# Input norms from token rows on ScalarE, an early spread of the bias table with a late read, and memory keys and values evacuated later

## The chip, the core and the metric

The kernel runs on one core of a Trainium2 chip. The metric is the time of one execution on the device, in microseconds (us), as a median of several runs. The engines are TensorE (PE, with PEld for its weight loads), VectorE (DVE), ScalarE (ACT), GpSimd (POOL) and SyncE (SP), whose queue issues nearly all DMAs here.

## What is computed

Two layers of an encoder trunk over 256 tokens of width 2048, in float32:

```
for l in range(DEPTH):                       # DEPTH = 2
    h = rms_norm(x, norm_mix[l])
    proj = h @ w_in[l]                       # 10 blocks of 512 columns and 32 gate columns
    gla_out = gla_mixer(g_q, g_k, g_v, g_r, gates)
    dil_out = dilated_mixer(d_q, d_k, d_v, rel_table)        # relative bias from a table (32, 4)
    kv = rms_norm(mem, mem_norm[l]) @ w_mem_kv[l]            # memory keys and values, 512 columns each
    mem_out = memory_mixer(m_q, kv)
    x = x + concat(gla_out, dil_out, mem_out) @ w_out[l]
    h = rms_norm(x, norm_mlp[l])
    x = x + square(relu(h @ w_up[l])) @ w_down[l]            # hidden width 8192
return rms_norm(x, norm_final)
```

The factor 1 / rms belongs to a token, so it can be applied to a product after the matmul; the kernel does so when it moves products out of PSUM (L257, `evac`).

## The kernel before

Every product with a weight block of 512 columns is one call of `linear` (L221). It goes through the 2048 rows of the weights in four quads of 512 rows. A quad is loaded as a tile `raw` of 1 MB (L211, three buffers), ScalarE casts it to a high part `wh` (L232), VectorE subtracts that to get the low part `wl` (L233; four buffers of half a quad for each part), and 24 matmuls follow (L250 to L252), 96 in one call. So the load of a quad goes out when the low part of the quad three before it is done, and the casts run at most two quads ahead of TensorE.

The order of the first layer's start: gains; quads of transposed memory `memT`, each split into `mem0qh` and `mem0ql` (L154, L155), between the quads of `w_mem` block 0 (memory keys); then `w_mem` block 1 (memory values); then `w_in` block 9 (memory queries), block 0, block 1 and so on. The transposed input `xT` is loaded and split the same way (L196, planned by L552). `ColumnNorm` (L104) gets 1 / rms from these transposed quads: GpSimd squares each (L113), adds them up (L115, L120), four matmuls against a vector of ones add over partitions (L122), and GpSimd takes the power (L83). `RowNorm` (L86) does it from token rows: ScalarE squares 512 columns of 128 tokens with a running sum (L95).

The relative-bias table: a matmul makes `rows`, 4 heads on 4 partitions (L284). `late_constants` (L287) is called after `w_in` block 0 and is queued on SP behind that block's last quad. It loads `ident`, `tri` and `masks`, writes `rows` 128 times for each head to the DRAM tensor `scr` (L295), and reads it back skewed into `bt` (L303). The whole of `x` by tokens is loaded behind it in one DMA (L593).

The program is ordered by a scheduler that goes by priority in the order of tracing; `tc.issue_after(ins)` queues what is traced in it behind `ins` on that engine. Each engine, and SP's queue, runs its instructions in the order that is so fixed. Tiles of one tag are handed out in the order of tracing: `xT` tiles share the ring with `km`, and come after it.

Of the kernel before, what the change touches and what calls it, by code (L numbers as in the profile page):

```python
# [11 lines left out]
F32 = mybir.dt.float32  # L12
# [3 lines left out]
ALU = mybir.AluOpType  # L16
AX = mybir.AxisListType
PSUM = bass.MemoryType.PSUM
# [24 lines left out]
def trunk_kernel(ctx: ExitStack, tc: tile.TileContext, a: dict):  # L43
# [23 lines left out]
    ones = const.tile([P, 1], F32, name="ones")  # L67
    nc.gpsimd.memset(neghalf, -0.5)
    nc.gpsimd.memset(ones, 1.0)
# [16 lines left out]
    class RowNorm:  # L86
        """Sums of squares by chunks of 512 columns, then 1 / rms of every token."""
# [16 lines left out]
    class ColumnNorm:  # L104
        """1 / rms of every token of a transposed input."""

        def __init__(self, name):
            self.name = name
            self.sums = slot([4, S], "sums_" + name)

        def add(self, q, v):
            o = self.sums if q == 0 else slot([4, S], "sq_" + self.name)
            nc.gpsimd.tensor_tensor(o, v, v, ALU.mult)  # L113
            if q:
                nc.gpsimd.tensor_tensor(self.sums, self.sums, o, ALU.add)  # L115

        def done(self):
            ps, v = aux([NT], "ss_" + self.name), self.sums
            for n in (2, 1):
                nc.gpsimd.tensor_tensor(v[:, :n], v[:, :n], v[:, n:2 * n], ALU.add)  # L120
            for t in range(NT):
                nc.tensor.matmul(  # L122
                    ps[:, t:t + 1], v[:, 0, t * P:(t + 1) * P], ones, start=True, stop=True
                )
            ss = small.tile([P, NT], F32, tag="ss2", name="ss_" + self.name)
            nc.vector.tensor_copy(ss, ps)
            return rstd(ss, NT, D, self.name)

    def turn_blocks(o, v):
        """o[f, kk, token] = v[token % 128, token // 128, 128 * kk + f], by blocks of 32 x 32"""  # L130
        src = v.rearrange("p t (b c) -> p t b c", b=4)
        dst = o.rearrange("p b (t s) -> p t b s", t=NT)
        for f in range(0, P, 32):
            for s in range(0, P, 32):
                yield nc.vector.transpose(
                    dst[f:f + 32, :, :, s:s + 32], src[s:s + 32, :, :, f:f + 32]
                )
# [24 lines left out]
    def split_T(v, quad, gain, name):  # L162
        """v: [P, NT, 512] of tokens; its transpose times gain, in two float32r parts"""
        h, l = new_parts(name)
        for j2 in range(2):
            ps = aux([2, S], name + "ps")
            for j in range(2):
                c = (2 * j2 + j) * P
                for t in range(NT):
                    nc.tensor.transpose(ps[:, j, t * P:(t + 1) * P], v[:, t, c:c + P], ident)  # L170
            parts_of(h, l, ps, j2, quad, gain)
        return h, l

    def split_turned(v, quad, gain, name, lhs, steps=(0, 8, 8)):
        """The same on DVE, in steps that run between the splits of weights."""
        o = turned_slot(name + "o")
        yield from paced(turn_blocks(o, v), steps)
        h, l = new_parts(name)
        for j2 in range(2):
            parts_of(h, l, o[:, 2 * j2:2 * j2 + 2, :], j2, quad, gain)  # L180
        lhs[quad] = h, l

    def heads_turned(v, name, heads):
        """The transpose alone, of all heads."""
        o = slot([H, S], name)
        yield from paced(turn_blocks(o, v), (0, 4, 4, 4, 4))
        heads[name] = o

    def turn(n=None):
        """Emits the next steps of the transposes on DVE."""  # L190
        while turning and n != 0:
            if next(turning[0], True):
                turning.popleft()
            n = n and n - 1

    def split_loaded(v, src, quad, gain, name, lhs, norm=None, pieces=1):  # L196
        """The parts of an input that lies transposed in memory; v is where it is loaded to."""
        n = 4 // pieces
        for c in range(0, 4, n):
            nc.sync.dma_start(v[:, c:c + n], src[quad, :, c:c + n])  # L200
            yield
        h, l = new_parts(name)
        for j2 in range(2):
            parts_of(h, l, v[:, 2 * j2:2 * j2 + 2, :], j2, quad, gain)
        lhs[quad] = h, l
        if norm is not None:
            norm.add(quad, v)
# [13 lines left out]
    def linear(wsrc, lhs, quads, loaded=()):  # L221
        """lhs: dict quad -> (hi, lo); returns the PSUM tiles of both token tiles."""
        ps = [ps_mm.tile([P, NW], F32, tag="mm", name=f"mm{t}") for t in range(NT)]
# [62 lines left out]

    def late_constants():  # L287
        nc.sync.dma_start(ident, a["ident"])
        tri32 = work.tile([P, 4, 320], F32, tag="E", name="tri32")
        nc.sync.dma_start(tri32, a["tri"])  # L290
        nc.vector.tensor_copy(tri, tri32)
        masks32 = slot([2, H, P], "masks32", mybir.dt.int32)
        nc.sync.dma_start(masks32, a["masks"])
        nc.vector.tensor_copy(masks, masks32)
        nc.sync.dma_start(  # L295
            scr[:, :, :NW], rows.rearrange("h (o j) -> h o j", o=1).to_broadcast([H, P, NW])
        )
        for h in range(H):
            v = bass.AP(
                tensor=scr.tensor, offset=scr.offset + h * P * SKEW + P - 1,  # L300
                ap=[[SKEW - 1, P], [1, S + P]],
            )
            nc.sync.dma_start(bt[:, h, :], v)  # L303

    def attend_weights(qT, kT, bias, name):
        """The softmax over the 256 keys, not yet divided by its sums, keys on partitions."""
# [33 lines left out]
    def attend_out(weights, v, name):  # L340
        """The attention's sum over the values, then the per-head RMS norm; [P, NT, 512]."""
# [80 lines left out]
    def gla_weights(qT, kT, gates):  # L422
# [3 lines left out]
        for d in range(2):  # L426
            qd = slot([NT, H, P], f"qd{d}")
            cr = slot([2, H, P], f"cr{d}")
            for i in range(NT):
# [24 lines left out]
                # the side that is a source of the other half holds keys, the other queries  # L454
# [22 lines left out]
                # forward blocks go where the sum is wanted, backward ones are added to them  # L477
# [55 lines left out]
    mem_norm, xnorm = ColumnNorm("mem"), ColumnNorm("mix")  # L533
    loaded, splits = [], {}
    for q in range(4):
# [3 lines left out]
            turned_slot(f"mem0{q}"), a["memT"], q, gains[:, 3, 0, :], f"mem0{q}", mem_lhs, mem_norm, n  # L539
# [5 lines left out]
        if q == 0:  # L545
            next(splits[key], None)
        else:
            pending.append(lambda key=key: next(splits[key], None))
    nc.sync.dma_start(rel, a["rel"])
    nc.sync.dma_start(onehot, a["onehot"])  # L550

    def plan_loads(name, loads, src, gain, lhs, norm=None):  # L552
        """Loads some quads after each of the next quads of weights, and splits one."""

        def step(i):
            for q in loads[i] if i < len(loads) else ():
                splits[name, q] = split_loaded(
                    slot([4, S], f"{name}{q}"), src, q, gain, f"{name}{q}", lhs, norm
# [9 lines left out]
    for l in range(DEPTH):  # L568
        w = a["w_in"]
        ps = linear(a["w_mem"][l, 0], mem_lhs, range(4), loaded if l == 0 else ())  # L570
        if l == 0:
            flush()
            bias_products()
            mem_rs = mem_norm.done()
            plan_loads("x0", ((0, 1), (2,), (3,)), a["xT"], gains[:, 0, 0, :], xlhs, xnorm)
        km = evac(ps, mem_rs, f"km{l}")
        heads = {}
        turning.append(split_turned(km, "km", None, f"kmT{l}", heads, (0, 4, 4, 4, 4)))
        ps = linear(a["w_mem"][l, 1], mem_lhs, range(4))
        vm = evac(ps, mem_rs, f"vm{l}")  # L580
        col = lambda i: linear(w[l, i], xlhs, range(4))
        ps = col(9)
        flush()
        rs = xnorm.done()
        rsq = small.tile([P, NT], F32, tag="rsq", name="rsq")
        nc.vector.tensor_scalar(rsq, rs, scale, None, ALU.mult)
        mq = evac(ps, rsq, "mq")
        turning.append(split_turned(mq, "mq", None, f"mqT{l}", heads))
        gq = evac(col(0), rsq, "gq")
        if l == 0:  # L590
            with tc.issue_after(newest[0]):
                late_constants()
                nc.sync.dma_start(x, a["x"].rearrange("(t p) d -> p t d", p=P))  # L593
# [3 lines left out]
        gk = evac(col(1), rs, "gk")  # L597
# [117 lines left out]
def _constants():  # L715
# [5 lines left out]
    # row r is a gate's position, a column an exponent's: sums over the gates between  # L721
# [18 lines left out]
def _blocks(w, width):  # L740
    """[L, K, N] -> [L, N / width, 128, K / 128, width]"""
# [6 lines left out]
def _turned(v):  # L748
    """[1, S, D] -> [D / 512, 128, 4, S]"""
# [47 lines left out]
```

## Time and profile before

| | us |
|---|---|
| median of 3 runs (2260.66 to 2263.08) | 2260.94 |
| span of the profiled execution | 2262.0 |
| TensorE busy in it | 2200.8 (97%) |
| VectorE busy | 1618.6 (72%) |
| ScalarE busy | 1124.2 (50%) |
| GpSimd busy | 71.1 (3%) |

A busy TensorE is not TensorE at its peak, since matmuls are pipelined: the records of neighbouring matmuls overlap. The distance between their starts is what one costs. Where an engine sits idle, the profile names what ended the idle time.

### The profile page before, as it was taken

How to read it: one execution, taken by the hardware profiler on the slowest of the kernel's cores; microseconds unless marked ns; L12 is line 12 of the kernel's file. 1: busy time of each engine (PE TensorE's matmuls, PEld its weight loads, DVE VectorE, ACT ScalarE, POOL GpSimd, SP SyncE). 2: the span in 40 equal slices, each digit the busy share in tenths (PEclk: the TensorE clock that was granted, in tenths of full speed). 3: DMA queues.
4: the chain of work that ended last, by engine and by line, in shares of the span. 5: the costliest groups of instructions: out<-in, count | busy, mean ns of one | idle time of the engine just before them, and what ended most of it. 6: DMA issues, size and time to landing. Idle time of an engine off the chain costs nothing.

```text
span 2262.0 us, 25763 instructions
## 1 busy us (share of the span) xinstructions
PE 2200.8 (97%) x9906; PEld 1823.4 (81%) x9906; DVE 1618.6 (72%) x2234; ACT 1124.2 (50%) x1497; POOL 71.1 (3%) x78
## 2 busy tenths in 40 slices
PE   7849999999999999999999999999999999999998
PEld 5638888888888888888888888888888888888886
DVE  7827787888567557657987677888864864765774
ACT  5426456555345445445654554655543543543543
POOL 4200000000000000000000000000000000000000
PEclk9979999999999999999999999999999999999999
DMA  6554445555555555555665443555555555555563
GB/s 250 166 161 150 168 146 171 189 202 186 198 193 188 203 186 196 195 188 203 211 206 195 170 153 135 178 186 191 194 194 201 188 191 199 186 201 190 189 220 130
DMA packets 62502, 421.16 MB, mean 186 GB/s; under 512 B 6923, under 2 KB 8203, under 8 KB 13356
## 3 DMA queue, kind: packets, MB, share of 16 engines
q1 hardware_dynamic: 62380, 419.53, 54.8%
q8 instruction: 77, 1.26, 0.2%
q14 instruction: 45, 0.37, 0.1%
HBM read 416.35 MB, written 3.15 MB: 185 GB/s over the span
## 4 chain that ended last, share of the span: by engine, by line
PE 95%; DMA 2%; DVE 2%; issue 0%; ACT 0%; SPq 0%; POOL 0%; ACTq 0%; POOLq 0%; DVEq 0%
PE mm L251 30%; PE mm L252 30%; PE mm L250 30%; DMA raw<-in_w_in 2%; DVE wl L233 1%; PE pv L350 1%; PE go L506 1%; PE pT L336 0%; DMA mem<-in_memT 0%; PE dg L466 0%; PE cum L435 0%; DVE x01l L155 0%; PE dg L470 0%; PE cum L436 0%; DVE x00l L155 0%
## 5 line engine op out<-in xcount | busy, mean ns | idle before, releaser
L233 DVE TENSOR_TENSOR wl<-raw,wh 128x1024 fp32r<-128x1024 f32 (+1 forms) x774 | 938.4, 1227 | 550.1 <-ACT wh L232 545.1
L232 ACT ACTIVATE wh<-raw 128x1024 fp32r<-128x1024 f32 (+1 forms) x774 | 814.3, 1054 | 889.8 <-PE mm L252 800.3
L252 PE MATMUL mm<-wh,uT0h 128*128 128x512 f32 x256 | 99.7, 389 | 0.0
L252 PE MATMUL mm<-wh,uT2h 128*128 128x512 f32 x256 | 99.7, 389 | 0.0
L252 PE MATMUL mm<-wh,zT1h 128*128 128x512 f32 x256 | 99.7, 389 | 0.0
L251 PE MATMUL mm<-wl,zT2h 128*128 128x512 f32 x256 | 99.7, 389 | 0.0
L251 PE MATMUL mm<-wl,uT3h 128*128 128x512 f32 x256 | 99.7, 389 | 0.0
L251 PE MATMUL mm<-wl,uT2h 128*128 128x512 f32 x256 | 99.7, 389 | 0.0
L252 PE MATMUL mm<-wh,zT0h 128*128 128x512 f32 x256 | 99.7, 389 | 0.0
L252 PE MATMUL mm<-wh,uT3h 128*128 128x512 f32 x256 | 99.7, 389 | 0.0
L251 PE MATMUL mm<-wl,zT0h 128*128 128x512 f32 x256 | 99.6, 389 | 0.0
L252 PE MATMUL mm<-wh,uT1h 128*128 128x512 f32 x256 | 99.6, 389 | 0.0
L251 PE MATMUL mm<-wl,uT0h 128*128 128x512 f32 x256 | 99.6, 389 | 0.0
L250 PE MATMUL mm<-wh,zT0l 128*128 128x512 f32 x256 | 99.6, 389 | 0.0
L252 PE MATMUL mm<-wh,zT3h 128*128 128x512 f32 x256 | 99.6, 389 | 0.0
L251 PE MATMUL mm<-wl,zT3h 128*128 128x512 f32 x256 | 99.6, 389 | 0.0
L250 PE MATMUL mm<-wh,zT1l 128*128 128x512 f32 x256 | 99.6, 389 | 0.0
L251 PE MATMUL mm<-wl,zT1h 128*128 128x512 f32 x256 | 99.6, 389 | 0.0
L251 PE MATMUL mm<-wl,uT1h 128*128 128x512 f32 x256 | 99.6, 389 | 0.0
L252 PE MATMUL mm<-wh,zT2h 128*128 128x512 f32 x256 | 99.6, 389 | 0.0
L250 PE MATMUL mm<-wh,uT1l 128*128 128x512 f32 x256 | 99.5, 389 | 0.0
L250 PE MATMUL mm<-wh,uT3l 128*128 128x512 f32 x256 | 99.3, 389 | 0.0
(447 smaller groups left out, 4721.6 us busy)
## 6 DMA issues: line engine op xcount, KB each, us to landing
raw<-in_w_up SPq DMA_DIRECT2D x128, 1024.0 KB, 4.9
raw<-in_w_down SPq DMA_DIRECT2D x128, 1024.0 KB, 4.9
raw<-in_w_in SPq DMA_DIRECT2D x80, 1024.0 KB, 5.0
raw<-in_w_out SPq DMA_DIRECT2D x32, 1024.0 KB, 4.9
raw<-in_w_mem SPq DMA_DIRECT2D x13, 1024.0 KB, 5.0
mem<-in_memT SPq DMA_DIRECT2D x7, 512.0 KB, 5.8
raw<-in_w_mem SPq DMA_DIRECT2D x12, 256.0 KB, 6.3
x<-in_xT SPq DMA_DIRECT2D x4, 512.0 KB, 6.7
```

Source lines behind the costliest of these rows:

```text
L232: nc.scalar.activation(hi, raw[:, k:k + n], AF.Copy)
L233: cut = nc.vector.tensor_tensor(lo, raw[:, k:k + n], hi.bitcast(F32), ALU.subtract)
L250: nc.tensor.matmul(ps[t], xl[:, kk, sl], hi, start=first, stop=False)
L251: nc.tensor.matmul(ps[t], xh[:, kk, sl], lo, start=False, stop=False)
L252: nc.tensor.matmul(ps[t], xh[:, kk, sl], hi, start=False, stop=last)
L350: nc.tensor.matmul(ps[:, h, :], pT[s][:, h, t * P:(t + 1) * P], v[:, s, h * P:(h + 1) * P], start=s == 0, stop=s == NT - 1,)
L506: nc.tensor.matmul(ps[:, j, :], AT[s][:, t, 2 * c + j, :], v[c][:, s, j * DV:(j + 1) * DV], start=s == 0, stop=s == NT - 1,)
```

## The change

- `ColumnNorm` and its vector of ones are gone. Both input norms of the first layer are a `RowNorm`. Memory by tokens is a new input, loaded in four DMAs of 512 columns into the tile of `x`, behind the last piece of the third quad of `w_mem` block 0; `ident` follows. ScalarE squares each chunk, and a DMA on GpSimd's queue then loads the same chunk of `x` over it; ScalarE squares that too.
- The quads of `memT` take tiles of the ring in place of two buffers of their own.
- `w_mem` block 1 accumulates in the other PSUM pool. The memory keys and values are evacuated after `w_in` block 9, the memory queries after block 0; `xT` loads are planned ahead of block 1 of `w_mem`, as before, but `km` is no longer traced in front of them.
- The write of `scr` (`spread_bias`) is queued on SP behind the last quad of `w_mem` block 1. `late_constants` keeps `tri`, `masks` and the reads of `bt`.
- In both layers the memory attention is traced behind `w_in` block 1 instead of in front of it.

```diff
-    class ColumnNorm:
-        def add(self, q, v):
-            o = self.sums if q == 0 else slot([4, S], "sq_" + self.name)
-            nc.gpsimd.tensor_tensor(o, v, v, ALU.mult)
-            if q:
-                nc.gpsimd.tensor_tensor(self.sums, self.sums, o, ALU.add)
...
-    def linear(wsrc, lhs, quads, loaded=()):
-        ps = [ps_mm.tile([P, NW], F32, tag="mm", name=f"mm{t}") for t in range(NT)]
+    def linear(wsrc, lhs, quads, loaded=(), pool=ps_mm, tag="mm"):
+        ps = [pool.tile([P, NW], F32, tag=tag, name=f"mm{t}") for t in range(NT)]
...
+    def spread_bias():
+        nc.sync.dma_start(
+            scr[:, :, :NW], rows.rearrange("h (o j) -> h o j", o=1).to_broadcast([H, P, NW])
+        )
+
     def late_constants():
-        nc.sync.dma_start(ident, a["ident"])
...
-        nc.sync.dma_start(
-            scr[:, :, :NW], rows.rearrange("h (o j) -> h o j", o=1).to_broadcast([H, P, NW])
-        )
...
-    mem_norm, xnorm = ColumnNorm("mem"), ColumnNorm("mix")
+    mem_norm, xnorm = RowNorm("mem"), RowNorm("mix")
...
-            turned_slot(f"mem0{q}"), a["memT"], q, gains[:, 3, 0, :], f"mem0{q}", mem_lhs, mem_norm, n
+            slot([4, S], f"mem0{q}"), a["memT"], q, gains[:, 3, 0, :], f"mem0{q}", mem_lhs, n
...
+    tokens = lambda v, c: v.rearrange("(t p) d -> p t d", p=P)[:, :, c * NW:(c + 1) * NW]
     nc.sync.dma_start(rel, a["rel"])
     nc.sync.dma_start(onehot, a["onehot"])
+    with tc.issue_after(newest[0]):
+        for c in range(4):
+            nc.sync.dma_start(x[:, :, c * NW:(c + 1) * NW], tokens(a["mem"], c))
+        nc.sync.dma_start(ident, a["ident"])
...
+        ps_k = linear(a["w_mem"][l, 0], mem_lhs, range(4), loaded if l == 0 else ())
         if l == 0:
             flush()
             bias_products()
+            plan_loads("x0", ((0, 1), (2,), (3,)), a["xT"], gains[:, 0, 0, :], xlhs)
+            ps_v = linear(a["w_mem"][l, 1], mem_lhs, range(4), pool=ps_ax, tag="ax")
+            with tc.issue_after(newest[0]):
+                spread_bias()
+
+            def memory_squares(c):
+                squares_of_x(mem_norm, c)
+                nc.gpsimd.dma_start(x[:, :, c * NW:(c + 1) * NW], tokens(a["x"], c))
+
+            pending.extend([lambda c=c: memory_squares(c) for c in range(4)])
+            ps_q = col(9)
+            flush()
             mem_rs = mem_norm.done()
+            km = evac(ps_k, mem_rs, f"km{l}")
+            vm = evac(ps_v, mem_rs, f"vm{l}")
+            keys_turned()
+            pending.extend([lambda c=c: squares_of_x(xnorm, c) for c in range(4)])
+            ps_g = col(0)
+            flush()
+            rs = xnorm.done()
+            nc.vector.tensor_scalar(rsq, rs, scale, None, ALU.mult)
+            mq = evac(ps_q, rsq, "mq")
+            queries_turned()
+            gq = evac(ps_g, rsq, "gq")
+            with tc.issue_after(newest[0]):
+                late_constants()
...
+        ps_gk = col(1)
         turn()
         o_mem = attend_out(attend_weights(heads["mq"], heads["km"], None, "mem"), vm, "memo")
         turning.append(heads_turned(gq, "gqT", heads))
-        gk = evac(col(1), rs, "gk")
+        gk = evac(ps_gk, rs, "gk")
```

## Rows read from the trace of the kernel before

**Rows 1.** Page, the span in 40 slices: busy tenths of TensorE, and its granted clock.

```profile
PE   7849999999999999999999999999999999999998
PEclk9979999999999999999999999999999999999999
```

**Rows 2.** Waits of TensorE, whole span: line waited for, us in total, times, longest.

```profile
PE mm L250 <- ACT wh L232: 34.4, 2, 29.1
PE mm L251 <- DVE wl L233: 13.3, 5, 8.5
PE mm L250 <- DVE mem02l L155: 3.8, 1, 3.8
```

**Rows 3.** Windows: stretch, its length, busy us (instructions) of PE, PEld, DVE, ACT, POOL; granted clock, DMA share, GB/s.

```profile
0.00:10.00 10.00, 4.62 (x11) 3.61 (x12) 3.97 (x7) 5.20 (x9) 2.42 (x9) 1.00 0.70 216
10.00:20.00 10.00, 6.47 (x22) 4.58 (x21) 10.00 (x8) 8.29 (x17) 8.38 (x5) 0.89 1.04 389
52.00:72.00 20.00, 12.66 (x56) 10.14 (x54) 19.87 (x19) 10.25 (x18) 18.13 (x9) 0.93 0.32 132
102.00:104.00 2.00, 2.00 (x10) 1.65 (x10) 1.65 (x3) 0.92 (x2) 0.00 (x0) 1.00 0.84 337
104.00:106.00 2.00, 2.00 (x11) 1.65 (x10) 1.95 (x5) 0.45 (x1) 0.00 (x0) 1.00 0.27 46
126.00:144.00 18.00, 0.00 (x0) 0.00 (x0) 0.00 (x0) 0.00 (x0) 0.00 (x0) 0.53 0.24 28
```

**Rows 4.** Timeline of VectorE: start, duration, line, operation, tiles, count.

```profile
57.62 9.23 DVE L155 SCALAR_TENSOR_TENSOR x00l<-x,gains,x00h 128x256 fp32r<-128x256 f32 x4
74.97 1.67 DVE L155 SCALAR_TENSOR_TENSOR x02l<-x,gains,x02h 128x256 fp32r<-128x256 f32 x4
```

**Rows 5.** Timeline of GpSimd, the last work of the input norm.

```profile
69.12 2.19 POOL L120 TENSOR_TENSOR sums_mix<-sums_mix 128x512 f32<-128x512 f32 x2
```

**Rows 6.** Timeline of SP's queue; the duration is that of the issue.

```profile
97.57 0.33 SPq L218 DMA_DIRECT2D raw<-in_w_in  x1
98.89 0.77 SPq L295 DMA_DIRECT2D scr<-rows  x1
99.71 7.64 SPq L593 DMA_DIRECT2D x<-in_x  x1
107.45 13.93 SPq L218 DMA_DIRECT2D raw<-in_w_in  x1
144.27 1.76 SPq L303 DMA_DIRECT2D bt<-scr  x4
```

**Rows 7.** Timeline of ScalarE: the cast after its long wait.

```profile
151.77 2.00 ACT L232 ACTIVATE wh<-raw 128x1024 fp32r<-128x1024 f32 x2 [36.78 <-DMA raw<-in_w_in]
```

**Rows 8.** Timeline of TensorE around the long wait, and the first use of the quad loaded at 97.57.

```profile
100.46 0.39 PE L250 MATMUL mm<-wh,x00l 128*128 128x512 f32 x1
116.78 0.61 PE L250 MATMUL mm<-wh,x03l 128*128 128x512 f32 x2
122.22 0.28 PE L265 MATMUL sc<-kmT0h,mqT0l 128*128 128x256 f32 x1
152.88 0.79 PE L250 MATMUL mm<-wh,x00l 128*128 128x512 f32 x1 [29.06 <-ACT wh L232]
```

**Rows 9.** DMA issues: tile, count, KB each, median us from issue to landing.

```profile
raw<-in_w_mem SPq DMA_DIRECT2D x13, 1024.0 KB, 5.0
mem<-in_memT SPq DMA_DIRECT2D x7, 512.0 KB, 5.8
x<-in_x SPq DMA_DIRECT2D x1, 2048.0 KB, 49.5
```

**Rows 10.** Groups by form on ScalarE: squares of rows; the reading of their sums.

```profile
L95 ACT ACTIVATE junk<-x 128x512 f32<-128x512 f32 x32 | 20.1, 629 | 40.6 <-DVE x L529 40.6
L95 ACT ACTIVATION_READ_ACCUMULATOR junk<-x 128x1 f32 x32 | 6.0, 186 | 0.0
```

**Rows 11.** Timeline of VectorE: the first output of the memory attention.

```profile
175.49 0.69 DVE L364 TENSOR_TENSOR memo<-pv,cmb 128x512 f32<-128x512 f32 x1
```

More of the change, by code (lines that the diff above doesn't have):

```diff
@@ L66, in trunk_kernel @@
     neghalf = const.tile([P, 8], F32, name="neghalf")
-    ones = const.tile([P, 1], F32, name="ones")
     nc.gpsimd.memset(neghalf, -0.5)
-    nc.gpsimd.memset(ones, 1.0)
     warm = small.tile([P, 1], F32, name="warm", bufs=1)
@@ L102, in done @@
             return rstd(ss, n, D, self.name + ("" if t is None else str(t)))
-    class ColumnNorm:
-        def __init__(self, name):
-            self.name = name
-            self.sums = slot([4, S], "sums_" + name)
-        def add(self, q, v):
-            o = self.sums if q == 0 else slot([4, S], "sq_" + self.name)
-            nc.gpsimd.tensor_tensor(o, v, v, ALU.mult)
-            if q:
-                nc.gpsimd.tensor_tensor(self.sums, self.sums, o, ALU.add)
[L117 to L123, printed above, removed]
-                )
-            ss = small.tile([P, NT], F32, tag="ss2", name="ss_" + self.name)
-            nc.vector.tensor_copy(ss, ps)
-            return rstd(ss, NT, D, self.name)
     def turn_blocks(o, v):
@@ L194, in turn, with split_loaded @@
             n = n and n - 1
-    def split_loaded(v, src, quad, gain, name, lhs, norm=None, pieces=1):
+    def split_loaded(v, src, quad, gain, name, lhs, pieces=1):
         n = 4 // pieces
@@ L205, in split_loaded @@
         lhs[quad] = h, l
-        if norm is not None:
-            norm.add(quad, v)
     newest = [None]
@@ L294, in late_constants @@
         nc.vector.tensor_copy(masks, masks32)
-        nc.sync.dma_start(
-            scr[:, :, :NW], rows.rearrange("h (o j) -> h o j", o=1).to_broadcast([H, P, NW])
-        )
         for h in range(H):
@@ L548, in trunk_kernel, with plan_loads @@
             pending.append(lambda key=key: next(splits[key], None))
+    tokens = lambda v, c: v.rearrange("(t p) d -> p t d", p=P)[:, :, c * NW:(c + 1) * NW]
     nc.sync.dma_start(rel, a["rel"])
     nc.sync.dma_start(onehot, a["onehot"])
-    def plan_loads(name, loads, src, gain, lhs, norm=None):
+    with tc.issue_after(newest[0]):
+        for c in range(4):
+            nc.sync.dma_start(x[:, :, c * NW:(c + 1) * NW], tokens(a["mem"], c))
+        nc.sync.dma_start(ident, a["ident"])
+    def plan_loads(name, loads, src, gain, lhs):
         def step(i):
@@ L557, in step @@
                 splits[name, q] = split_loaded(
-                    slot([4, S], f"{name}{q}"), src, q, gain, f"{name}{q}", lhs, norm
+                    slot([4, S], f"{name}{q}"), src, q, gain, f"{name}{q}", lhs
                 )
@@ L569, in trunk_kernel, with keys_turned, queries_turned @@
         w = a["w_in"]
-        ps = linear(a["w_mem"][l, 0], mem_lhs, range(4), loaded if l == 0 else ())
+        heads = {}
+        col = lambda i: linear(w[l, i], xlhs, range(4))
+        def keys_turned():
+            turning.append(split_turned(km, "km", None, f"kmT{l}", heads, (0, 4, 4, 4, 4)))
+        def queries_turned():
+            turning.append(split_turned(mq, "mq", None, f"mqT{l}", heads))
+        ps_k = linear(a["w_mem"][l, 0], mem_lhs, range(4), loaded if l == 0 else ())
+        rsq = small.tile([P, NT], F32, tag="rsq", name="rsq")
         if l == 0:
@@ L573, in trunk_kernel @@
             bias_products()
-            mem_rs = mem_norm.done()
[L575 to L590, printed above, removed]
+            plan_loads("x0", ((0, 1), (2,), (3,)), a["xT"], gains[:, 0, 0, :], xlhs)
+            ps_v = linear(a["w_mem"][l, 1], mem_lhs, range(4), pool=ps_ax, tag="ax")
+            with tc.issue_after(newest[0]):
+                spread_bias()
@@ L591, in trunk_kernel @@
+            ps_g = col(0)
[5 more added lines that the diff above has]
+            gq = evac(ps_g, rsq, "gq")
             with tc.issue_after(newest[0]):
                 late_constants()
-                nc.sync.dma_start(x, a["x"].rearrange("(t p) d -> p t d", p=P))
+        else:
+            km = evac(ps_k, mem_rs, f"km{l}")
+            keys_turned()
+            vm = evac(linear(a["w_mem"][l, 1], mem_lhs, range(4)), mem_rs, f"vm{l}")
+            ps_q = col(9)
+            flush()
+            rs = xnorm.done()
+            nc.vector.tensor_scalar(rsq, rs, scale, None, ALU.mult)
+            mq = evac(ps_q, rsq, "mq")
+            queries_turned()
+            gq = evac(col(0), rsq, "gq")
@@ L769 @@
         "xT": _turned(i["x"]),
+        "mem": i["mem"].reshape(S, D),
         "memT": _turned(i["mem"]),
```

## The prediction

> **What bounds the kernel now.** I read the slices first: TensorE is at its full tenths everywhere but in the first three slices of 56.6 us and the last, and the granted clock dips only in the third [rows 1]. So whatever this change is worth is decided in the first 160 us; the 2100 us behind them are TensorE's own matmuls. Then TensorE's waits: all of them lie in that start, 34.4 us for casts of weights by ScalarE, 29.1 of it in one piece, and 13.3 and 3.8 us for VectorE [rows 2]. They have two causes.
>
> The first is VectorE slowed beside GpSimd. From 52 to 72 us GpSimd is busy 18.13 of 20 us, VectorE 19.87, and TensorE only 12.66 [rows 3]. Four subtractions of a split take 9.23 us there; as soon as GpSimd's last add ends at 71.3 us [rows 5] the same four take 1.67 us [rows 4]. DMA was at a share of 0.32 in that stretch, so it is not DMA that slows them.
>
> The second is the wait of 29.06 us up to 152.88 us [rows 8]. ScalarE waits 36.78 us for a quad of weights, to 151.77 [rows 7]; its load was issued at 107.45 us [rows 6] and so took some 44 us. It was not waiting on a slot or a semaphore: it had been issued. Right in front of it on SP's queue stand the write of `scr` (98.89 us) and the load of `x` (99.71) [rows 6]. During the stall the DMA share is 0.24, that is 3.9 of 16 engines, at 28 GB/s [rows 3]. The write has 4 heads as its outer dimension, and 4 engines carry it. `scr` has landed at 144.27 us, when its read goes out [rows 6]; `x` has at 99.71 + 49.5 = 149.2 us [rows 9], the quad at 151.7. That is the order of the queue: each engine serves SP's transfers in turn, so a quad that needs all 16 engines waits for the four that carry `scr`. Its duration: the rate falls from 337 to 46 GB/s about 103.5 us [rows 3], when what was ahead is through; to 144.27 that is 40.8 us.
>
> **The change, part by part.**
>
> *Squares off GpSimd.* GpSimd's squares and sums go, and with them the slow VectorE: quads are then cast as fast as they arrive. ScalarE gets for each of memory and x eight squares of 0.629 us and eight sum reads of 0.186 [rows 10], 6.5 us, 13.0 together. They cost TensorE nothing as long as casts stay ahead; ScalarE was busy 8.29 us of 10 at its fullest there [rows 3], and it will stand idle in the stall described next. If that cover fails the most they cost is those 13.0 us.
>
> *More to load early.* Up to the write of `scr` SP now issues memT 2048 KB, block 0 and block 1 of `w_mem` 8192 KB, memory by tokens 2048 KB, xT 2048 KB and some 190 KB of small ones: about 14,530 KB = 14.9 MB (the sizes of one in [rows 9], memory by tokens taken at that of `x`). The `xT` quads stood behind the first quad of block 9 because their tiles come after `km`; `km` is now traced later, so they go ahead of `scr`. At 216 GB/s in the first 10 us, 2.2 MB move, and the remaining 12.7 MB take 32.7 us at 389 GB/s [rows 3]. So the last quad of `w_mem` is in at about 42.7 us. Its issue waits for the low part of the quad three before, the first of block 1, which lands about 30 us and takes 2 casts and 2 subtractions: at some 34 us, an estimate, and it doesn't decide. The last quad of block 0 is now behind memory by tokens, 8.6 MB in, so it lands about 27 us and TensorE waits some 4 us for it; I cost that at nothing, because it is covered by what comes now.
>
> *The write of `scr` early.* It is the same statement, so the same 4 engines and 40.8 us, now queued right behind the last quad of `w_mem`: on the engines from 42.7 to 83.5 us. Behind it on the queue stands the first quad of block 9. What TensorE has by then is its prefetch: the quad issued at 97.57 was used at 116.78 [rows 6, 8], so about 19 us of work lie between issue and use, far less than 40.8. The last quad of `w_mem`, issued at 34, is used at 53 and done 5 us later: TensorE runs dry at about 58 us and waits, as it did at 123.8, only in front of block 9 and not of block 1. The quad lands 2.5 us behind `scr` (149.2 to 151.7 before, [rows 7, 9]), and the first matmul is 1.1 us behind its cast's start (151.77 to 152.88) [rows 7, 8]: 83.5 + 2.5 + 1.1 = 87.1 us.
>
> *`x` on GpSimd's queue.* 2048 KB that in the old order took 144.27 to 149.2 = 4.9 us on the four engines behind `scr`. The trace has no second queue busy beside SP's. The bounds are 0 (if these loads come when `scr` is done and fill gaps) and 4.9 us (if they share the four engines with it or come in front). The squares of memory need only tokens that land about 24 us, and ScalarE has gaps from then on, so the loads come early: I take 4.9. The first matmul of block 9 is then at 92.0 us. The Trainium skill, "DMA: Bandwidth & Descriptors", section "Queues, rings and completion order", says that an engine takes turns between the queues it has work for; by that the loads would mix with `scr`, and the sum would be the same 92.0. No run here shows it yet.
>
> *Read of `bt` late.* SP stood 22.9 us at it before (121.38, the end of the issue in front, to 144.27 [rows 6]), but behind a load that was held anyway. It comes behind the last quad of block 0, some 35 us after `scr` has landed: nothing.
>
> *Later evacuation and attention.* The new holders of PSUM are freed by evacuations that need only the norms. Their inputs are there long before block 0 ends, since ScalarE runs ahead of TensorE. Moving the memory attention behind block 1 lets block 1 start without it; bounds nothing below, and above the largest wait that the trace shows outside the two causes, 3.8 us [rows 2]. I take nothing, as TensorE has other blocks to run beside it and shows no wait behind 160 us.
>
> **The sum.** Before, block 1 starts at 152.88 us, with the attention's scores already done, 1.6 us from 122.22 to the beginning of the wait [rows 8]. Now block 9 starts at 92.0. Blocks 9 and 0 take 2 x 21.76 us (100.46 to 122.22 for one, [rows 8]) = 43.5, so block 1 starts at 135.5, with 1.6 us of scores still to do. Both long waits are left at a low granted clock (0.53 on average from 126 to 144 us [rows 3]), so what that costs stands on both sides. 152.88 - 135.5 - 1.6 = 15.8 us, about 16. Against the span of 2262.0 us that gives 2246; the median of the runs lies 1.1 us below that span, so 2245 us.
>
> So of some 55 us of waits in the start 16 come back: the slow VectorE is gone, but where it cost its time TensorE now waits for `scr`. The two waits were one after the other; they now lie on top of each other.
>
> **Its range.** The transfers ahead of `scr` may move at 400 GB/s, or at 350 (start 41.9 or 46.4); `scr` may take 40.8, or 45.4 us if counted from its issue; `x` 0 or 4.9 us. Block 9 starts between 86.3 and 100.3 us: gain 21.7 to 7.7, time 2239 to 2253. A quad of block 9 that gets in front of `scr` on the queue would give up to 2.7 us more, the attention take 3.8: 2236 to 2257.
>
> **Rivals.**
> *The early write is hidden.* If loads aren't held behind it, block 9 starts when TensorE is through with `w_mem`, at 58 us and not at 92.0: 34 us earlier, 2245 - 34 = 2211. For it: SP's wait of 22.9 us at the read does go. Against it: a load held 44 us that had no wait left [rows 6, 7]. The Trainium skill, "DMA: Bandwidth & Descriptors", section "Rules for kernel authors", says to issue a DMA early and wait on its semaphore late, to overlap it with compute; by that rule it would come out so. This trace has the transfers behind pay. Chance 0.08.
> *Nothing gained.* The wait is as foreseen, but attention behind block 1 leaves TensorE waiting for it: its chain takes up to 22.6 us from the end of the stall to its first output, 152.88 to 175.49 [rows 8, 11], covered by block 1. If 12 to 20 of that stand uncovered in the one layer or the other, they eat the 16: 2257 to 2265, or 2261, within 0.2%. Chance 0.07.
> *Slower.* ScalarE's queue is in order. If squares of x are put in front of the cast of block 9's first quad, and the four loads of `x` come through the crowded engines only behind `scr`, one after another at 5.8 us (512 KB of memT, [rows 9]), the last lands at 83.5 + 4 x 5.8 = 106.7 us; the squares of that chunk, 1.6 us, and the cast's 1.1 us make 109.4, and with the other squares still to do, 6.5 us in all, 114.3: 22 us later than forecast, 2267. It decides from block 9 starting behind 108 us. Against it: the loads of `x` stand on another queue and wait only for the squares of memory, so most of them should be through before `scr` is. Chance 0.06.
>
> **Chances.** The forecast has 0.79. Faster by over 0.2% (4.5 us, about what a measurement of this kernel can tell from no change) has it and the first rival, 0.87; same 0.07; slower 0.06. The range is that of the forecast alone: it leaves 0.21 out, of which the upper end takes in a little of the second rival.
>
> **What would show it.** Right: splits of 1.7 us for four throughout; a DMA share near 0.24 for some 40 us from about 43 us; TensorE idle from some 58 to 92 us, waiting for ScalarE's cast on a load of `in_w_in`; no wait at 122 to 153. Wrong: block 9 starting before 80 us, or behind 101; a new wait of TensorE behind 135 us; VectorE slow with GpSimd idle.

## The result and the profile after

The changed kernel takes 2277.44 us as a median (2274.89 to 2278.83), the kernel before in the same comparison 2262.01 us (2260.66 to 2263.35). The ratio is 1.0065, with a 95% interval of 1.0051 to 1.008: it is slower by 15.4 us, where the prediction had it faster by 16. The profiled execution of after takes 2277.81 us, with a span of 2276.0.

The page of after, its totals of TensorE, VectorE, ScalarE and GpSimd and the 40 slices of TensorE:

```profile
PE 2203.2 (97%) x9898; PEld 1822.8 (80%) x9898; DVE 1593.5 (70%) x2234; ACT 1133.8 (50%) x1529; POOL 38.2 (2%) x63
PE   7599999999999999999999989999999999999998
```

GpSimd and VectorE have less to do, as intended, and ScalarE about 10 us more. In the slices the weak ones at the start are two in place of three [rows 1], and one in the second layer is no longer full. The waits of TensorE over the whole span (line waited for: us in total, times, longest):

```profile
PE mm L221 <- ACT wh L203: 35.7, 5, 27.3
PE mm L222 <- DVE wl L204: 25.6, 7, 9.7
```

The waits between 180 and 400 us, and under the dots those between 1180 and 1500 us, where before had none at all:

```profile
PE mm L222 <- DVE wl L204: 12.4, 2, 9.7
...
PE mm L222 <- DVE wl L204: 11.2, 2, 9.7
```

The long wait for ScalarE's cast is still there at its old size [rows 2], and 23.6 us of waits for VectorE are new, half of them in each layer. They lie in the 2100 us that the prediction had set aside.

**The start.** Timelines of TensorE, ScalarE and SP's queue in after (start, duration, engine, line, operation, tiles, count, and in brackets the idle time in front and what ended it):

```profile
91.19 1.22 PE L221 MATMUL mm<-wh,x00l 128*128 128x512 f32 x2 [27.26 <-ACT wh L203]
...
87.53 1.70 ACT L127 ACTIVATE x03h<-x,gains 128x256 fp32r<-128x256 f32 x4 [31.56 <-DMA x<-in_xT]
90.08 2.00 ACT L203 ACTIVATE wh<-raw 128x1024 fp32r<-128x1024 f32 x2 [0.85 <-DMA raw<-in_w_in]
...
35.55 0.78 SPq L259 DMA_DIRECT2D scr<-rows  x1
36.37 21.43 SPq L173 DMA_DIRECT2D x<-in_xT  x1
57.91 55.40 SPq L189 DMA_DIRECT2D raw<-in_w_in  x8
113.84 2.20 SPq L275 DMA_DIRECT2D bt<-scr  x4
```

Block 9 starts at 91.19 us; the prediction had 92.0. Behind the write of `scr` stands the last quad of `xT`, whose issue alone is held up for 21.43 us, and ScalarE waits for it until 87.53. The reads of `bt` go out without a wait. The rates in that stretch (window, its length, busy us of PE, PEld, DVE, ACT, POOL; granted clock, DMA share, GB/s):

```profile
42.00:44.00 2.00, 0.73 (x2) 0.30 (x2) 0.84 (x1) 1.93 (x3) 0.00 (x0) 1.00 1.05 438
46.00:60.00 14.00, 12.84 (x50) 9.85 (x49) 9.14 (x17) 9.96 (x24) 0.90 (x2) 0.90 0.33 54
60.00:76.00 16.00, 3.93 (x18) 2.92 (x16) 0.00 (x0) 0.00 (x0) 0.00 (x0) 0.69 0.70 178
76.00:84.00 8.00, 0.00 (x0) 0.00 (x0) 0.00 (x0) 0.00 (x0) 0.00 (x0) 0.50 0.23 28
```

All engines of the DMA are full until some 45 us; then the rate falls, to a mean of 54 GB/s, while SP stands at the issue of `xT`. It rises from 58 us, with the loads of block 9 that go out from 57.91, and at 76 to 84 us it is 28 GB/s at a share of 0.23, as during the stall before [rows 3]. By the prediction's own sum block 1 then begins two blocks of 21.76 us later, at 134.7, plus the 1.6 us of scores that now come behind it: 152.88 - 134.7 - 1.6 = 16.6 us gained at that point [rows 8]. In the trace it begins at 137.64, because the first matmuls of block 9 run at a low granted clock (0.50 from 92 to 96 us); the kernel before pays about the same behind 152.88 (0.50 from 152 to 156 us), so 16.6 stands.

**Behind it.** Timelines of VectorE and TensorE in the first layer of after, from block 3 into block 6:

```profile
214.91 1.22 DVE L391 TENSOR_TENSOR gl<-z,gh 128x1024 fp32r<-128x1024 f32 x1
216.05 7.18 DVE L108 STREAM_TRANSPOSE gqT<-gq 32x256 f32<-32x256 f32 x16
223.25 7.20 DVE L108 STREAM_TRANSPOSE gkT<-gk 32x256 f32<-32x256 f32 x16
231.10 3.49 DVE L204 TENSOR_TENSOR wl<-raw,wh 128x1024 fp32r<-128x1024 f32 x3
...
232.37 0.80 PE L222 MATMUL mm<-wl,x00h 128*128 128x512 f32 x1 [9.68 <-DVE wl L204]
232.96 0.63 PE L223 MATMUL mm<-wh,x00h 128*128 128x512 f32 x1
233.39 0.63 PE L222 MATMUL mm<-wl,x00h 128*128 128x512 f32 x1
```

VectorE turns queries `gq` and keys `gk` of the gated mixer in 32 transposes without a single cast between them, 14.4 us. The low parts of three half quads wait behind these, and TensorE waits 9.68 us for the first. When it starts again its matmuls are 0.43 us apart where the full rate is 0.23 (from 237.19 to 237.42), and go on so for 4 us. The granted clock of these stretches:

```profile
228.00:232.00 4.00, 0.00 (x0) 0.00 (x0) 3.88 (x8) 0.00 (x0) 0.00 (x0) 0.50 0.00 0
232.00:236.00 4.00, 3.63 (x9) 2.86 (x10) 3.96 (x7) 0.00 (x0) 0.00 (x0) 0.50 0.68 219
236.00:240.00 4.00, 4.00 (x18) 3.29 (x17) 3.97 (x7) 1.34 (x2) 0.00 (x0) 0.92 0.75 309
```

0.50 is the lower of the two levels, 1.2 GHz of 2.4. So a layer loses 12.4 or 11.2 us of waits and about 2 us of clock. Two layers make 27.6 us, and 16 minus that is -12: about the sign and size of the result.

### The profile page after: what moved, and what is told of

The parts are those of the page before. It is cut to its first block, busy times and chain, and to the rows that moved or that the text cites. A ratio compares the mean times of both kernels' runs of the same rounds, so it can differ in the third digit from the quotient of the medians.

```text
span 2276.0 us, 25766 instructions
## 1 busy us (share of the span) xinstructions
PE 2203.2 (97%) x9898; PEld 1822.8 (80%) x9898; DVE 1593.5 (70%) x2234; ACT 1133.8 (50%) x1529; POOL 38.2 (2%) x63
## 4 chain that ended last, share of the span: by engine, by line
PE 92%; DVE 3%; DMA 3%; ACT 1%; issue 1%; SPq 0%; POOL 0%; ACTq 0%; POOLq 0%; DVEq 0%
PE mm L222 29%; PE mm L223 29%; PE mm L221 29%; DMA raw<-in_w_in 1%; DMA raw<-in_w_mem 1%; PE pv L322 1%; PE go L478 1%; DVE gqT L108 1%; DVE wl L204 1%; DVE gkT L108 1%; PE pT L308 0%; DVE dkT0o L108 0%; DMA x<-in_mem 0%; DVE dkT1o L108 0%; PE dg L438 0%
## 5 line engine op out<-in xcount | busy, mean ns | idle before, releaser
L204 DVE TENSOR_TENSOR wl<-raw,wh 128x1024 fp32r<-128x1024 f32 (+1 forms) x774 | 928.5, 1215 | 574.9 <-ACT wh L203 570.5
```

The source lines that it names most:

```text
L204: cut = nc.vector.tensor_tensor(lo, raw[:, k:k + n], hi.bitcast(F32), ALU.subtract)
```

## Experiments

The times of the kernel before that stand beside the experiments are 2262.72 us (the first four), 2263.14 (the next four) and 2264.08 (the last three). So where two kernels stand beside different ones of these, up to 1.4 us of their difference is that drift, and up to 2.1 us against the changed kernel, which stands beside 2262.01. The theory after the result: **A**, the start gained what was foreseen, and the attention moved behind block 1 costs some 27 us in the two layers. The rival **B**: that move is innocent, and what is lost comes with the start's new order.

### The attention back in front

```diff
-        ps_gk = col(1)
         turn()
         o_mem = attend_out(attend_weights(heads["mq"], heads["km"], None, "mem"), vm, "memo")
         turning.append(heads_turned(gq, "gqT", heads))
-        gk = evac(ps_gk, rs, "gk")
+        gk = evac(col(1), rs, "gk")
```

> The changed kernel with one part undone: in both layers the memory attention is traced in front of block 1 again, as before the change. Theory A (the loss is the one run of 32 transposes on VectorE, 14.4 us, that the later place of the attention leaves in each layer): no wait of TensorE behind 135 us, no run of more than 16 transposes, and 2277 - 2 x 12.5 to 15 = 2246 to 2252 us. Rival B (the later evacuation of keys, values and queries crowds VectorE in the first layer, whatever the attention does): layer 2 gets its 13 us back, layer 1 doesn't, some 2263 us.

Measured 2249.96 us, ratio 0.9939 (0.9925 to 0.9954). The waits of TensorE:

```profile
PE mm L221 <- ACT wh L203: 34.9, 4, 25.5
PE mm L222 <- DVE wl L204: 3.6, 5, 1.7
```

Two lines of the program give back 27.5 us, and the waits for VectorE go from 25.6 to 3.6 us. The start stays as it was. So the other parts of the change together are worth 12.8 us.

### The write of `scr` from 128 partitions

```diff
-    rows = work.tile([P, NW], F32, tag="E", name="rows")[:H]
+    rel_wide = work.tile([P, NW], F32, tag="junk", name="rel_wide")[:BUCKETS + 1, :P]
+    rows = work.tile([P, NW], F32, tag="E", name="rows")
...
-        nc.tensor.matmul(ps, rel, onehot, start=True, stop=True)
+        nc.vector.tensor_copy(          # each head 32 times
+            rel_wide.rearrange("b (h r) -> b h r", h=H),
+            rel.rearrange("b (h o) -> b h o", o=1).to_broadcast([BUCKETS + 1, H, 32]),
+        )
+        nc.tensor.matmul(ps, rel_wide, onehot, start=True, stop=True)
...
-            scr[:, :, :NW], rows.rearrange("h (o j) -> h o j", o=1).to_broadcast([H, P, NW])
+            scr.rearrange("h (r s) w -> (h r) s w", s=4)[:, :, :NW],
+            rows.rearrange("p (o j) -> p o j", o=1).to_broadcast([P, 4, NW])
```

The same bytes go to the same place, but 128 partitions, not 4, write them, and the outer dimension is 128, not 4; the two change together, and no run tells them apart. This was put into three kernels: the changed one (attention late), the one of the first experiment (attention in front), and the kernel before.

> The changed kernel with the bias rows made on 128 partitions (32 copies of each head by the matmul), so that the write of scr goes out from 128 partitions and with an outer dimension of 128 in place of 4; the attention stays late. Theory: the write takes some 3 us and not 41, block 9 starts at about 60 us in place of 91.2, and the whole is 2277 - 29 = 2248 us. Rival (TensorE is held at block 9 by the loads of x and the squares as well): block 9 starts behind 75 us and less than 15 us come back.

> Both edits together: attention in front, and the write of scr from 128 partitions. If the two losses are independent: 2246 - 29 = 2217 us, faster than both kernels. If the freed start runs into the next limit (16 transposes in one piece, weights still loading), 2225 to 2235.

> The kernel before with nothing but the write of scr from 128 partitions. Theory (loads stand behind the write on its four engines): the wait of 29 us in front of block 1 is gone, 2262 - 30 = 2232 us. Rival (SP's wait at the read of bt holds up the loads): the read still stands behind the write on SP, and more than half of the 29 us stay.

Measured: 2247.19 us (ratio 0.9927, 0.9912 to 0.9942), 2218.54 us (0.9803, 0.9786 to 0.9819) and 2232.94 us (0.9865, 0.9851 to 0.988). Waits of TensorE with the attention late:

```profile
PE mm L222 <- DVE wl L204: 23.9, 4, 9.7
PE mm L221 <- ACT wh L203: 9.9, 2, 5.1
```

With the attention in front (the largest):

```profile
PE mm L221 <- ACT wh L203: 10.3, 2, 5.4
```

In the kernel before with the wide write:

```profile
PE mm L251 <- DVE wl L233: 9.6, 3, 8.4
PE mm L250 <- ACT wh L232: 5.6, 1, 5.6
PE mm L250 <- DVE mem03l L155: 3.7, 1, 3.7
```

The timeline of VectorE in that one:

```profile
55.76 9.24 DVE L155 SCALAR_TENSOR_TENSOR x00l<-x,gains,x00h 128x256 fp32r<-128x256 f32 x4
```

The wide write is worth 30.3, 31.4 and 29.8 us: nearly the same in all three. The wait of 25 to 29 us for ScalarE's cast is gone from each. Block 9 starts at 63.90 and 61.84 us in the first two, where about 60 was expected; the write takes 10.7 and 12.6 us there from issue to landing, and not the 3 us expected of it. What is left in the kernel before, 8.4 and 3.7 us for VectorE among it, is the start that GpSimd slows: the four splits of `x00l` still take 9.24 us. Between the third kernel and the second lie 14.4 us, which is about what the other parts of the change bring once the write no longer hides them. The kernel with the attention in front and the wide write beats both kernels, the one before by 2%.

### Where the write stands

The first experiment and its form with the wide write, each with the write put back behind block 0, in front of the reads of `bt`:

```diff
-            with tc.issue_after(newest[0]):
-                spread_bias()
...
         nc.vector.tensor_copy(masks, masks32)
+        spread_bias()
```

> The kernel of the first experiment (attention in front of block 1 again, 2249.96 us), with the narrow write of scr put back where it stood in the kernel before, behind block 0's last quad and directly in front of the reads of bt. Theory A (the write costs about the same wherever it stands, as TensorE has only some 19 us of work between the issue and the use of a load; early it merely covered what the slow VectorE had cost before): block 9 starts by 60 us, a wait of some 24 to 29 us for a cast by ScalarE in front of block 1 comes back, total 2243 to 2250 us. Rival B (the early place of the write is what the start gained): a loss of the start's 16 us, 2262 to 2268 us.

> The kernel of the third experiment (attention in front, scr written from 128 partitions, 2218.54 us), with that write put back behind block 0's last quad, in front of the reads of bt. Theory A (written from 128 partitions it takes a few us on all engines, so its place is worth little): 2218 to 2222 us. Rival B (the reads of bt behind it hold SP's queue until it lands, and the loads of block 1 with it): 2224 to 2230 us and a wait of TensorE of 5 us or more in front of block 1.

Measured: 2252.96 us for the narrow write (ratio 0.9952, 0.9937 to 0.9967) and 2218.29 us for the wide one (0.9798, 0.9782 to 0.9814). SP's queue in the first:

```profile
84.69 0.77 SPq L259 DMA_DIRECT2D scr<-rows  x1
...
129.66 0.33 SPq L276 DMA_DIRECT2D bt<-scr  x1
```

The longest wait of TensorE there:

```profile
PE mm L221 <- ACT wh L203: 38.9, 5, 28.8
```

SP's queue in the second:

```profile
83.30 0.64 SPq L264 DMA_DIRECT2D scr<-rows  x1
...
92.57 1.76 SPq L282 DMA_DIRECT2D bt<-scr  x4
```

Early or late makes 3.0 us with the narrow write and nothing with the wide one. The first was expected at 2250 at most and came out 3 us above; but the rival, by which the early place carries the start's gain, wanted 2262 at least. With the narrow write the read goes out 45 us behind the write, and TensorE waits 28.8 us once, as before the change; with the wide one it goes out 9.3 us behind it, and nobody waits.

### The late attention alone, in the kernel before

The two lines of the first experiment, the other way round, in the kernel before: `ps_gk = col(1)` in front of the attention, `evac(ps_gk, rs, "gk")` behind it.

> The kernel before, with one part of the change alone: in both layers the memory attention, and with it the queueing of gq's transposes, behind block 1. Theory A (that part costs 12.5 to 14 us in each layer, by the run of 32 transposes): 2285 to 2291 us, with a new wait of TensorE of some 10 us for low parts in each layer. Rival B (it costs only together with the later evacuation of keys, values and queries): 2260 to 2266 us. In the first layer the chain of the attention is covered by block 1 in either.

Measured 2292.53 us, ratio 1.0127 (1.0112 to 1.0142): 29.4 us slower, 14.7 for a layer on average, and 1.5 us above the upper end expected. VectorE in its first layer:

```profile
232.92 7.18 DVE L135 STREAM_TRANSPOSE gqT<-gq 32x256 f32<-32x256 f32 x16
240.13 7.19 DVE L135 STREAM_TRANSPOSE gkT<-gk 32x256 f32<-32x256 f32 x16
```

The waits of TensorE between 180 and 400 us, of which the kernel before had none:

```profile
PE mm L251 <- DVE wl L233: 11.2, 2, 9.7
```

The same picture without any other part of the change. Rival B, and with it the later evacuation of keys, values and queries as a cause, falls.

### What in the late attention costs the time

With the attention, the queueing of `gq`'s transposes is moved too, and the gates come behind both. VectorE in the kernel before, where 12 of the 16 run beside block 1:

```profile
176.10 5.36 DVE L135 STREAM_TRANSPOSE gqT<-gq 32x256 f32<-32x256 f32 x12
```

In after they start only when the gates' last step `gl` has begun (216.05 and 214.91). Their steps are put between the casts of whatever block is traced next, which is now block 2 and no longer block 1; and their tile belongs to the ring that the gates' tiles use, and now comes after these. The runs don't tell these two reasons apart. The first kernel puts the queueing alone back, and both with it:

```diff
+        turning.append(heads_turned(gq, "gqT", heads))
         ps_gk = col(1)
         turn()
         o_mem = attend_out(attend_weights(heads["mq"], heads["km"], None, "mem"), vm, "memo")
-        turning.append(heads_turned(gq, "gqT", heads))
         gk = evac(ps_gk, rs, "gk")
```

> The changed kernel, with the memory attention left behind block 1; only the queueing of gq's transposes is put back in front of block 1, so that their ring tile is asked for ahead of the gates' tiles and their turns run between the casts of block 1. Theory A (what costs time in each layer is that VectorE runs the 32 transposes of gq and gk in one piece, and TensorE waits 9.7 us for the low parts of weights behind them; the attention itself costs nothing where it stands): no more than 16 in one piece, no wait of TensorE above 5 us for low parts behind 100 us, and the 27.5 us of the first experiment come back: 2248 to 2254 us. Rival B (the attention behind block 1 is itself the cost, by its evacuations and scores between the blocks): 2270 to 2278 us. Half and half, about 2263, would say that both are.

Measured 2263.1 us (ratio 0.9999, 0.999 to 1.0009): 14.3 us better than the changed kernel, and 13 worse than with the attention in front. Half, so neither theory was enough. Its longest wait of TensorE between 180 and 400 us, and under the dots the longest between 1180 and 1500 us, in the second layer:

```profile
PE mm L221 <- ACT gv L231: 5.2, 1, 5.2
...
PE mm L222 <- DVE wl L204: 3.9, 2, 3.7
```

ScalarE in the first of these stretches:

```profile
222.47 1.99 ACT L390 ACTIVATE gh<-z 128x1024 fp32r<-128x1024 f32 x2
224.36 2.40 ACT L231 ACTIVATE gv<-mm,r_mix 128x512 f32<-128x512 f32 x4
```

In the first layer TensorE now waits for an evacuation of `gv` out of PSUM, which stands on ScalarE behind the gates' last cast; and `gkT` still comes in one piece of 16, at 228.51. In the second it waits 3.7 us for the low parts that stand behind that piece of 16 (1320.65 to 1327.84). Two kernels were to tell these apart. One asks for the tile of `gkT` in front of the gates, the other traces the gates in front of the attention:

```diff
+        turning.append(heads_turned(gk, "gkT", heads))
+        turn(1)
         gates = log_gates(xlhs, rs, l)
-        turning.append(heads_turned(gk, "gkT", heads))
```

> The fifth experiment (2263.1 us; gq's transposes queued in front of block 1, attention behind it) with gk's transposes also asked for ahead of the gates' tiles. Of the 27.5 us that the first experiment gave back, that one gave 14; the question is where the other 13 lie. Theory C (the tile of gkT still comes behind the gates' tiles, so that its 16 transposes, 7.2 us, stand between two casts): 2250 to 2256 us. Rival D (16 transposes in one piece are borne, as in the first experiment, where TensorE waits 1.7 us for them; the rest is that gates and attention both fall behind block 1, so that ScalarE and VectorE come late to an evacuation or a cast): 2260 to 2266 us, with a wait for an evacuation of ScalarE left.

```diff
-        o_mem = attend_out(attend_weights(heads["mq"], heads["km"], None, "mem"), vm, "memo")
         gk = evac(ps_gk, rs, "gk")
         gates = log_gates(xlhs, rs, l)
+        o_mem = attend_out(attend_weights(heads["mq"], heads["km"], None, "mem"), vm, "memo")
         turning.append(heads_turned(gk, "gkT", heads))
```

> The fifth experiment (2263.1 us) with the gates traced in front of the memory attention, still both behind block 1. Theory D (what is left of the cost is the gates' chain of elementwise steps behind the attention, which the products of the gated mixer need at once behind block 3): with the gates first, no wait of 5.2 us for gv's evacuation, and 2250 to 2256 us. Rival C (the 16 transposes of gkT in one piece): 2260 to 2266 us.

Measured: 2266.8 us (ratio 1.0013, 1.0003 to 1.0022) and 2254.48 us (0.9962, 0.9947 to 0.9977). The longest wait of TensorE between 180 and 400 us in the first, and under the dots between 1180 and 1500 us:

```profile
PE mm L221 <- ACT gv L231: 5.3, 1, 5.3
...
PE mm L222 <- DVE wl L204: 5.4, 2, 5.2
```

In the second, between 180 and 400 us:

```profile
PE sc L236 <- ACT dkT0h L121: 1.2, 1, 1.2
```

Asking earlier for `gkT` does not bring it earlier: it starts at 228.63 us in the first layer, and in the second at 1325.47, behind gates that are done later because more transposes of the attention's output `memo` now stand between their steps. So it is not the gates' tiles in the ring that hold `gkT`, and this kernel does not test what an earlier `gkT` is worth. The wait for `gv` stays, the one in the second layer grows to 5.2 us, and the whole is 3.7 us slower, 2.8 without the drift of the kernel before, and 0.8 us above rival D's range. With the gates first the wait for `gv` is gone, the one for low parts in the second layer shrinks to 0.2 us, and 8.6 us come back, though `gkT` is still one piece of 16 on VectorE there:

```profile
199.99 1.22 DVE L391 TENSOR_TENSOR gl<-z,gh 128x1024 fp32r<-128x1024 f32 x1
...
218.78 7.18 DVE L108 STREAM_TRANSPOSE gkT<-gk 32x256 f32<-32x256 f32 x16
```

The gates are done 18 us before `gkT`, with time left for the evacuations and casts behind them. So of the 27.5 us, 14.3 lie in the late queueing of `gq`'s transposes and 8.6 in the gates that the attention pushes back: in the first layer the evacuation of `gv` comes late behind them, in the second the low parts do, behind a `gkT` that follows the late gates at once. The last 4.5 us, up to the attention in front, were not told apart; the two waits of 1.2 us for `dkT` that this kernel has, one in each layer, are a part of them, and TensorE also waits 3.4 us more in the first 180 us (41.1 against 37.7), for which no run shows the cause. Against the kernel before that stands beside each, the three parts are 15.5, 9.6 and 3.2 us.

One more kernel asked whether the early request for `gkT` helps the best one, the attention in front with the wide write. There a `turn()` behind block 1 empties the queue of transposes first:

```diff
         gk = evac(col(1), rs, "gk")
+        turn()
+        turning.append(heads_turned(gk, "gkT", heads))
+        turn(1)
         gates = log_gates(xlhs, rs, l)
-        turning.append(heads_turned(gk, "gkT", heads))
```

> The third experiment (2218.54 us; attention in front of block 1, scr written from 128 partitions) with gk's transposes also queued in front of the gates. If the order of gk's transposes behind the gates costs anything where the attention stands in front, it is the one wait of 1.7 us in the first layer: 2214 to 2219 us. If not, 2218 to 2221.

Measured 2224.47 us (ratio 0.9827, 0.9813 to 0.9842), 5.9 us slower than without it (4.6 without the drift) and outside both expectations. Here too `gkT` comes no earlier: it starts at 183.73 us, 4.0 us later than without the edit, with two pieces of transposes of `memo` now between the gates' steps. The wait of 1.7 us of TensorE for low parts became one of 4.2, and what else costs was not followed up:

```profile
PE mm L222 <- DVE wl L204: 5.8, 5, 4.2
```

## Why the prediction was wrong

*Squares off GpSimd.* Right. Four subtractions take 1.67 us from the first quads on, by VectorE's timeline of after:

```profile
13.61 1.67 DVE L128 SCALAR_TENSOR_TENSOR mem01l<-mem,gains,mem01h 128x256 fp32r<-128x256 f32 x4
```

*More to load early.* Right in size: transfers run at 438 GB/s from 42 to 44 us and the fall comes at about 45; the prediction had 42.7. It was wrong about the order: the last quad of `xT` went out behind the write, not in front of it, and instead the four loads of `x` came before it. They are issued between 22.62 and 28.49 us on GpSimd's queue, the write at 35.55. The two changes nearly cancel, which is luck.

*The write of `scr` early.* Right in the wait and its end. It is on the engines from some 45 us to some 84, when the rate begins to rise again, TensorE is dry from 63.9 us (91.19 - 27.26) where 58 was foreseen, and block 9 starts at 91.19 instead of 92.0. The load that holds ScalarE longest is another one than foreseen: the last quad of `xT` (31.56 us), with the first weights of block 9 only 0.85 us behind its split. The wide write shows that the narrow form is the cause: with the wide write TensorE is busy for all of 60 to 100 us, by the windows of the kernel with the attention late:

```profile
60.00:100.00 40.00, 40.00 (x178) 33.11 (x178) 26.17 (x36) 18.69 (x21) 0.00 (x0) 1.00 0.63 223
```

The Trainium skill, "DMA: Bandwidth & Descriptors", section "Rules for kernel authors", says that an outermost dimension smaller than 16 confines a DMA to at most that many engines, and that the 128 partitions should stand there. The runs agree, with 45.4 us from issue to landing in the kernel before (98.89 to 144.27 [rows 6]) against 12.6 in the kernel with the attention in front and the wide write, and some 30 us of the whole time. The row of the second, KB and us from issue:

```profile
scr<-rows SPq DMA_DIRECT2D x1, 1024.0 KB, 12.6
```

The Trainium skill's rule to issue early and wait late, from the same section, showed little here: early against late is 3.0 us for the narrow write and nothing for the wide one.

*`x` on GpSimd's queue, read of `bt` late.* The read cost nothing, as foreseen. For `x` the prediction took 4.9 us behind `scr`; its 2 MB came ahead of `scr` instead, which at some 400 GB/s is about 5 us, an estimate. From 22.62 us on both queues had loads in flight, with 389 to 416 GB/s in all up to 38 us; how they share an engine no row shows.

*Later evacuation and attention.* This is the step that failed. The prediction took nothing, with 3.8 us as the upper bound; the term measured 27.5 us (2277.44 - 2249.96), and alone, in the kernel before, 29.4. The 3.8 us is the largest wait that the prediction saw outside its two causes. It is a wait for the split `mem02l` at 31.40 us, in the start that GpSimd slows, and so measures nothing of this step. And such a bound holds for the order that was traced, and the step changes that order. The chain of the attention was looked at, as the rival "nothing gained" did, and that chain costs TensorE little (at most the 4.5 us that are left with the gates first). What was overlooked is what is queued behind it: the transposes of `gq`, whose request the diff shows below `attend_out` in its context lines, and the gates. Before, `gqT` was turned beside block 1; now it comes behind the gates and runs with `gkT` in one piece on VectorE, in whose queue the low parts of the weights stand. What else moves with a step was asked of DMAs and not of VectorE. The cost also comes in each layer, where the prediction looked for the whole effect in the first 160 us.

*The sum.* The start is worth 12.8 us by the first experiment, against 15.8 predicted; at block 1 it was 16.6, of which a part is lost again, 1.7 us in a wait for VectorE behind it in the first experiment; what takes the other 2 us is not shown. The 32.4 us between 2245 and 2277.4 so lie nearly all in the one term: 27.5 from the attention, 3.0 from the start, and 1.1 from the runs of before, 2262.0 here and 2260.9 there. The statement that the two waits of the start come to lie on top of each other held: taken out of the kernel before one after the other, the write gives 29.8 us and the rest 14.4; the change took out the second alone.

*The rivals.* The first, an early write that is hidden, did not occur with the narrow write; the wide one makes it come true, and with the attention in front 2218.54 us stand beside its 2211, and block 9's start at 61.84 us beside its 58. The second rival named the right place, the attention behind block 1, but let it eat 12 to 20 us in one of the layers through the attention's own latency; it takes about 14 in each, by the work behind it. The third, squares of `x` in ScalarE's queue, did not occur: block 9 didn't start behind 108 us.

## What to carry to other kernels

Before moving a block of a program whose queues follow the order of tracing, list everything that is traced or queued between its old and its new place, on each engine that the critical path needs, and look at the last of it and not only at the block. A bound that comes from "no wait here before" says nothing once that order is changed: count the work of VectorE and ScalarE that must now fit between two of the blocks. When a small transfer holds up a queue, change its shape before its place: here the shape was worth 30 us, and the place 3.

## What the runs showed of the hardware

A narrow write holds the loads behind it in two ways. SP stands at the issue of the next one, 21.43 us in after, and from 48 to 58 us only 25 to 27 GB/s move. And loads that go out come in late: from 60 to 76 us they move at 178 GB/s with a share of 0.70, and yet TensorE is busy for 3.93 of 16 us, and ScalarE has nothing to cast or split until 87.53. That each quad lacks the part that the crowded engines carry would explain it, and the 28 GB/s at a share of 0.23 that follow (3.7 of 16 engines) fit that; no row shows the engines one by one, so it is argued and not shown. And a wait of 9.7 us in the middle of the program costs more than itself: the granted clock is at 0.50 before its end and for 4 us behind it, in which matmuls start 0.43 us apart in place of 0.23, some 2 us each time.
